# A trunk layer on one core: the output projection in seven products, its operand resident, the mix passed through DRAM, stages queued as one

## The chip, the core and the metric

The kernel runs on one core of one Trainium2 chip. It is written so that each instruction goes to one engine's queue: TensorE (PE, matmuls and transposes into PSUM banks), VectorE (DVE), ScalarE (ACT), GpSimd (POOL) and SyncE (SP), which issues most DMAs. A queue is served in order; engines meet through semaphores. The order in a queue is not simply that of the program: a scheduler lays the instructions out ahead of time by priority, and `tc.high_priority(offset=n)` moves what is written under it forward by n instructions' worth of priority. The metric is device time in microseconds of one execution, as the median of several runs. Before the change it is 1659.52 us (three runs, 1656.72 to 1660.0).

## The reference

One layer of a hybrid encoder trunk, 1024 tokens by 1024 features, all float32. The part around the change:

```python
mix = (jax.nn.sigmoid(gate_ret + merge_gate_b[l, 0]) * y_a
       + jax.nn.sigmoid(gate_lru + merge_gate_b[l, 1]) * y_b)
x = x + mix @ w_out[l]

h = rms_norm(x, norm2_w[l])
up = h @ ffn_w_up[l]
gate, val = jnp.split(up, [D_FF], axis=-1)
gate = causal_depthwise_conv(gate, ffn_conv_w[l], ffn_conv_b[l])
x = x + (jax.nn.gelu(gate) * val) @ ffn_w_down[l]
```

Ahead of it come an input projection with 28 column groups, a retention branch of four heads (y_a) and a recurrent branch with convolution and scan, the LRU (y_b). After it comes the last norm.

## The kernel before

**Precision.** [...] A product takes three passes, high by high, high by low and low by high (`PASSES`, line 129). A 128x128 block by a 128x512 row block is three matmuls.

**Units.** A projection is cut into jobs. A job has a left operand of four blocks A11, A12, A21, A22 (each 128 rows by four 128-wide pieces of k) and a right operand of sets B11 to B22 (each four tiles j of 128x512), which stays in SBUF for all jobs of the stage. A plain job (`mm_std`, line 346) makes the four quarters (m, h) of its output in 8 block products of 12 matmuls, 96 in all. A fast job (`mm_fast`, line 407) is Strassen's scheme in the form with seven products, 84 matmuls; it needs sums of A blocks (S1 to S4, made in `preps`, lines 265 to 291) and of B sets (T1 to T4, made once per stage). After a product that the scheme uses twice, ScalarE copies the bank out (L432, in `keep`), and VectorE adds what belongs together (L438, L443).

**Queues of work written out by hand.** `loads` (line 224) loads A blocks in the order of the list `queue`, and `preps` splits them; `pump` (line 296) drives both ahead of the products, up to seven blocks (`NBLK`). `builders` (line 307) is a list of generators that build right operands; `build` gives it a budget after each product, as long as 20 tiles of the pool U (81 tiles of 128x512) are free, and `need` forces it when a product lacks its set. `back` holds generators with background work of a stage (rotary, retention, LRU steps), driven by `advance`. `hp(SOON)` puts builders 400 ahead, `hp()` and `pump` 1500, the copies of `keep` and `total` 3000.

**Stages.** 28 jobs of the input projection; four plain jobs with w_ret_o (`emit_ret_o`); four with w_lru_o, the first plain, three fast (`emit_lru_o`, line 1068), whose output quarters are the rows of mix: channels 256n + 128m, tokens 512h. They stay in SBUF in `mixf`, 16 tiles. Then, lines 1194 to 1241, the output projection as plain loops: split the 16 tiles of mix; for each column half c load and split eight tiles of w_out, and for each of eight row tiles 24 matmuls (L1221), add x (L1223), store to `x1_d` (L1225). In the second column half each group of four row tiles goes through `norm_half` (line 533): the squares' sums, the scale per row (L537), 4 transposes per k tile (L543), and a split with the norm's weight (L547 to L553) into the operand `h2` of the next stage. Then 24 up jobs, the first plain (tokens in the free dimension, so `h2` sets B11 and B21 are tokens 0 to 511), with `post_ff` behind each, which stores gated channels into `ff_d` in blocks; the sums of h2 come from `tsets` (line 574). Then three groups of four down jobs: the A blocks are read from `ff_d`, the right operand w_dn is loaded by `operand` (line 1021), and its sums were made during the up stage by `down_sums` (line 1286), stored in `td_d` and read back by `down_op`. Each stage is appended to `queue` when its `run` is called (line 473).

`operand` holds a tile back until it has had time to land: `landed` (line 569) waits for two ticks (`LAG`), a tick being a call of `build`.

## Time and profile before

| what | value |
|---|---|
| runs | 1660.0, 1659.52, 1656.72 us; median 1659.52 |
| profiled execution | 1658.44 us; span from first to last instruction 1656.7 us |
| granted TensorE clock, mean | 0.997 |
| HBM | read 177.38 MB, written 67.11 MB |
| input projection, 0 to 653 us | TensorE busy 638.42 us, VectorE 531.38, ScalarE 393.02 |
| ret and LRU outputs, 653 to 844 | 186.51 of 191; 155.99; 110.32 |
| output projection, 844 to 938 | 92.75 of 94; 42.01; 22.46 |
| up, 938 to 1410 | 467.82 of 472; 372.45; 236.29 |
| down and end, 1410 to 1657 | 236.77 of 247; 185.22; 118.14 |

Times are microseconds from the first instruction. A row of a group reads: line, engine, operation, tiles written and read, shapes and count, then busy time and mean nanoseconds of one, then the idle time of the engine ahead of them with the instruction that ended most of it. A row of the timeline reads: start, length, engine, line, operation, count, and in brackets the idle time before it with its releaser. In the windows each engine has its busy time and its number of instructions; PEclk is the granted TensorE clock (1.00 is full), DMA the mean busy share of 16 DMA engines. Matmuls are pipelined, so a matmul's duration is longer than the distance between two of them.

### The profile page before, as it was taken

What the parts mean: (1) busy time and instruction counts of PE and PEld (TensorE: products, weight loads), DVE (VectorE), ACT (ScalarE), POOL (GpSimd) and SP (SyncE); (2) the same over time, 40 slices, a digit from 0 to 9 for tenths busy, and PEclk for the clock granted to TensorE, in tenths of its full rate; (3) what the DMA queues carried; (4) which work ended last, traced back from release to release, by engine and by line L of the source; (5) the groups of instructions that cost most, each with busy time, mean ns of one, the idle gap of its engine ahead of it and who ended that gap; (6) DMA issues with size and microseconds to landing.
All of it is one profiled execution on the core that took longest, in us unless ns stands there. A gap on an engine that the chain in (4) does not pass through costs nothing. (4 is left out here: it accounts for less than half of the span.)

```text
span 1656.7 us, 21338 instructions
## 1 busy us (share of the span) xinstructions
PE 1622.3 (98%) x7224; PEld 1329.8 (80%) x7224; DVE 1287.0 (78%) x2366; ACT 880.2 (53%) x1480; POOL 40.6 (2%) x60
## 2 busy tenths in 40 slices
PE   8999999999999998999999999999999999999997
PEld 6788888888888877888778778888888887888886
DVE  8998767676888888958871798777777767877786
ACT  7664444535677866853440464444444545453554
POOL 0001000000000000000000000000000000000000
PEclk9999999999999999999999999999999999999999
DMA  8243223131332337658462144444444456778761
GB/s 296 81 161 102 73 68 90 45 96 45 104 119 95 134 122 251 213 171 268 153 215 89 65 150 163 138 134 135 139 143 139 156 160 218 260 262 264 267 203 77
DMA packets 134350, 251.16 MB, mean 152 GB/s; under 512 B 15584, under 2 KB 15712, under 8 KB 134240
## 3 DMA queue, kind: packets, MB, share of 16 engines
q1 hardware_dynamic: 130016, 236.16, 43.9%
q0 software_dynamic: 4224, 13.64, 2.2%
q8 instruction: 56, 0.92, 0.2%
q14 instruction: 54, 0.44, 0.1%
HBM read 177.38 MB, written 67.11 MB: 148 GB/s over the span
## 5 line engine op out<-in xcount | busy, mean ns | idle before, releaser
L417 PE MATMUL g<-u,w 128*128 128x512 f32 x5124 | 1204.0, 393 | 14.9 <-ACT u L432 13.3
L417 PEld LDWEIGHTS g<-u,w 128*128 128x128 f32 x5124 | 958.2, 188 | 218.7 <-ACT u L432 18.6
L188 ACT CAST w<-w 128x512 fp32r<-128x512 f32 x471 | 291.3, 620 | 413.2 <-PE g L417 286.9
L189 DVE TENSOR_TENSOR w<-w,w 128x512 fp32r<-128x512 f32 x471 | 321.9, 684 | 83.4 <-ACT w L188 73.7
L360 PE MATMUL g<-u,w 128*128 128x512 f32 x960 | 223.5, 390 | 0.0
L360 PEld LDWEIGHTS g<-u,w 128*128 128x128 f32 x960 | 179.3, 188 | 38.0 <-ACT u L686 0.3
L443 DVE TENSOR_TENSOR u<-g,u 128x512 f32<-128x512 f32 x183 | 125.3, 685 | 50.5 <-PE g L417 40.4
L432 ACT COPY u<-g 128x512 f32<-128x512 f32 x183 | 106.1, 580 | 65.0 <-PE g L417 62.8
L122 DVE TENSOR_TENSOR u<-u,u 128x512 fp32r<-128x512 f32 (+1 forms) x192 | 122.0, 683 | 15.1 <-ACT u L122 10.4
L122 ACT CAST u<-u 128x512 fp32r<-128x512 f32 x160 | 90.4, 619 | 45.0 <-DVE u L122 15.3
L1221 PE MATMUL g<-u,u 128*128 128x512 f32 x384 | 90.0, 392 | 1.0 <-ACT u L188 0.9
L1221 PEld LDWEIGHTS g<-u,u 128*128 128x128 f32 x384 | 71.3, 188 | 16.6 <-ACT u L188 1.4
L1254 DVE SCALAR_TENSOR_TENSOR u<-u,par,u 128x511 f32<-128x511 f32 x96 | 71.6, 745 | 4.1 <-ACT u L1251 3.4
L1259 POOL DMA_DIRECT2D ff_d<-u x48 | 36.1, 752 | 1251.7 <-DVE u L1258 1251.7
L271 DVE TENSOR_TENSOR w<-w,w 128x512 f32<-128x512 f32 x61 | 42.0, 689 | 25.3 <-DMA w<-ff_d 9.6
L188 ACT CAST u<-u 128x512 fp32r<-128x512 f32 x72 | 43.3, 619 | 26.5 <-DMA u<-w_out 11.2
L1251 ACT ACTIVATE u<-u,par 128x512 f32<-128x512 f32 x48 | 39.2, 817 | 28.2 <-DVE u L443 27.5
L852 PE MATMUL a<-u,u 128*128 128x512 f32 x192 | 48.7, 393 | 2.5 <-ACT u L188 1.6
L189 DVE TENSOR_TENSOR u<-u,u 128x512 fp32r<-128x512 f32 x72 | 47.9, 683 | 4.0 <-ACT u L188 3.7
L1223 DVE TENSOR_TENSOR u<-g,u 128x512 f32<-128x512 f32 x16 | 10.9, 690 | 48.2 <-PE g L1221 48.2
L852 PEld LDWEIGHTS a<-u,u 128*128 128x128 f32 x192 | 35.5, 188 | 12.0 <-ACT u L188 3.1
L274 DVE TENSOR_TENSOR w<-w,w 128x512 f32<-128x512 f32 x61 | 41.9, 687 | 1.0
(175 smaller groups left out, 1211.7 us busy)
## 6 DMA issues: line engine op xcount, KB each, us to landing
w<-w_in SPq DMA_DIRECT2D x112, 256.0 KB, 2.7
w<-w_up SPq DMA_DIRECT2D x96, 256.0 KB, 2.7
u<-w_dn SPq DMA_DIRECT2D x96, 256.0 KB, 3.2
u<-x_d SPq DMA_DIRECT2D x56, 256.0 KB, 5.0
x_d<-u SPq DMA_DIRECT2D x48, 256.0 KB, 3.5
ff_d<-u POOLq DMA_DIRECT2D x48, 256.0 KB, 2.9
td_d<-u SPq DMA_DIRECT2D x48, 256.0 KB, 3.3
w<-ff_d SPq DMA_DIRECT2D x48, 256.0 KB, 4.3
```

The lines of the kernel that those rows point to most:

```text
L122: ins = fn(*args, **kw)
L188: S.copy(hi, src)
L189: V.tensor_sub(lo, src, hi.bitcast(F32))
L271: V.tensor_add(s1, a21, a22)
L274: V.tensor_sub(s1, s1, a11)
L360: PE.matmul(ps[h], w[a][:, c], o[b], start=n == 0, stop=n == 23)
L417: PE.matmul(bank, w[a][:, c], need(op, (bn, j))[b], start=first and n == 0, stop=n == 11, skip_group_check=True)
L432: BS.last = S.copy(u, bank).ins.name
L443: BV.last = V.tensor_add(u, bank, u).ins.name
L852: PE.matmul(ps, wg[g][a][:, cs], xs[k][b], start=q == 0, stop=q == 5)
L1221: PE.matmul(ps, o[a][:, 128 * t:128 * t + 128], wo[k][b], start=n == 0, stop=n == 23)
L1254: V.scalar_tensor_tensor(c[:, s:], src[:, :TH - s], w, c[:, s:], ALU.mult, ALU.add)
```

## The change

The output projection becomes a stage of jobs like the down stage. w_out is its right operand, resident in SBUF for all four jobs (tokens 256t + 128m are A's rows), with the sums T1 to T4 made during retention, stored to DRAM (`tw_d`) and read back. The quarters of mix are stored to DRAM in blocks (`mix_d`) and loaded as A blocks; a job's blocks are loaded only once the quarters are written out in the program (`ready`). The first job runs plain, in the new order `mm_by` "k" (all four quarters on k half 0, then all on half 1, in four banks); three are fast. The first up job runs `mm_by` "h" (token half 0 first). x1 goes to DRAM from each quarter, ScalarE squares it, and the norm becomes a generator, started after the third and the fourth output job, in the background. The up and down jobs are put into `queue` ahead of the output jobs' run.

```diff
+    def mm_by(jb, op):
+        r = range(2)
+        steps = ([(m, h, kh) for kh in r for m in r for h in r] if jb.by == "k" else
+                 [(m, h, kh) for h in r for kh in r for m in r])
...
+        for m, h, kh in steps:
+            an, bn = f"A{m + 1}{kh + 1}", f"B{kh + 1}{h + 1}"
...
+            pump((jb, an))
+            n = 0
+            for j in range(4):
+                c = slice(128 * j, 128 * j + 128)
+                o = need(op, (bn, j))
+                for a, b in PASSES:
+                    PE.matmul(banks[m, h], jb.blk[an][a][:, c], o[b], start=left[m, h] == 2 and n == 0,
+                              stop=left[m, h] == 1 and n == 11)
+                    n += 1
...
+            if not left[m, h]:
+                jb.emit(m, h, banks[m, h], None)
+                psg.put(banks[m, h])
+            build(BRATE)
+            advance(RATE)
...
     def loads():
...
             for nm in jb.order:
+                m, kh = int(nm[1]) - 1, int(nm[2]) - 1
+                while jb.ready is not None and not jb.ready(m, kh):
+                    yield None
                 t = W.get()
...
+    def out_w_sums(j):
+        def rd(kh, c):
+            t = get()
+            SY.dma_start(t, w_out[4 * kh + j, :, TH * c:TH * c + TH])
+            return t
+        b11, b12, b22 = rd(0, 0), rd(0, 1), rd(1, 1)
+        yield 1.0
+        V.tensor_sub(b11, b12, b11)
+        ST.dma_start(tw_d[0, j], b11)
+        V.tensor_sub(b12, b12, b22)
+        ST.dma_start(tw_d[2, j], b12)
+        put(b12)
+        b21 = rd(1, 0)
+        yield 1.0
+        V.tensor_sub(b22, b22, b11)
+        ST.dma_start(tw_d[1, j], b22)
+        put(b11)
+        yield 1.0
+        V.tensor_sub(b21, b21, b22)
+        ST.dma_start(tw_d[3, j], b21)
+        put(b21, b22)
...
+    def kept_sums(op, src):
+        def fetch(n, j):
+            t = get()
+            SY.dma_start(t, src[int(n[1]) - 1, j])
+            return t
+        keys = [(f"T{i}", j) for i in (1, 2, 3, 4) for j in range(4)]
+        for key, (tick, t) in zip(keys, reads(fetch, keys, AHEAD_B)):
+            yield from landed(tick)
+            op[key] = split(t, get, BS, BV)
+            put(t)
+            yield 0.6
...
             V.tensor_add(t, t, g)
             put(g)
-            mixf[ch, h] = t
+            ST.dma_start(mix_d[2 * h:2 * h + 2, :, ch // 4, :, ch % 4, :].rearrange("t m p c -> p (t m) c"),
+                         t.rearrange("p (q c) -> p q c", q=4))
+            put(t)
+            mixed.add((ch, h))
...
-            add(base + 2, emit_to(gg, AF.Silu, True), lambda hd=hd: ret_out(hd, dict(gg)))
+            add(base + 2, emit_to(gg, AF.Silu, True), lambda hd=hd: chain(ret_out(hd, dict(gg)), out_w_sums(hd)))
...
+    def emit_out(t, fast):
+        def emit(m, c, src, unit):
+            if fast and unit is not None:
+                acc = unit
+            else:
+                acc = wjobs[t].take(m, c)
+                V.tensor_add(acc, src, acc)
+                if unit is not None:
+                    put(unit)
+            i = 2 * t + m
+            ST.dma_start(x1_d[x_row(t, m, c)], acc)
+            j = psa.get()
+            S.activation(j, acc, AF.Square, accum_out=nst[:, c, i:i + 1])
+            psa.put(j)
+            if t == 3:
+                last4[m, c] = acc
+            else:
+                put(acc)
+        return emit
...
+            rstd_of(r, v, w)
+            if t >= 2:
+                return norm_half(t - 2)
...
+    def norm_half(half):
+        z = {}
+        for t in range(4):
+            i = 4 * half + t
+            for c in range(2):
+                z[t, c] = get()
+                if i < 6:
+                    SY.dma_start(z[t, c], x1_d[x_row(i // 2, i % 2, c)])
+        yield 1.0
...
+        for k in range(KT):
+            ps = psa.get()
+            for t in range(4):
+                c0 = 128 * (k % 4)
+                PE.transpose(ps[:, 128 * t:128 * t + 128], z[t, k // 4][:, c0:c0 + 128], ident)
+            w = pc("norm2_w", k)
+            hi, lo, f = get(F32R), get(F32R), get()
+            S.activation(hi, ps, AF.Copy, scale=w)
+            V.scalar_tensor_tensor(lo, ps, w, hi.bitcast(F32), ALU.mult, ALU.subtract)
+            S.activation(f, ps, AF.Copy, scale=w)
...
+            yield (0.5, 0.25)[half]
...
+        if half == 1:
+            builders.append(tsets(h2, lambda n, j: keep2[n, j], here=True))
...
+    def out_start():
+        builders.append(operand(wop, w_out_set, False, ("B11", "B12", "B21", "B22")))
+        builders.append(kept_sums(wop, tw_d))
+
+    wjobs = [Job(lambda m, kh, t=t: mix_d[t, m, kh].rearrange("p k c -> p (k c)"), wop,
+                 emit_out(t, t > 0), out_post(t), fast=t > 0, last=t == 3, drop12=t == 0,
+                 pre=((0, 0), (0, 1), (1, 1)), fetch=from_x(t), by=None if t else "k",
+                 order=None if t else ("A11", "A21", "A12", "A22"),
+                 ready=lambda m, kh, t=t: all((4 * kh + j, t // 2) in mixed for j in range(4)))
+             for t in range(4)]
+    ojobs[-2].post = out_start
+    queue.extend(wjobs)
...
+    ups = [Job(pair_src(w_up, i), h2, emit_to(gv), up_post(i), fast=i >= STD_U, last=i == NF - 1,
+               drop12=i == STD_U - 1, by="h" if i == 0 else None,
+               order=None if i else ("A11", "A21", "A12", "A22")) for i in range(NF)]
...
+                 ready=lambda m, kh, g=g: state["ff"] >= 8 * g + 4 * kh + 4)
              for g in range(3) for t in range(4)]
+    queue.extend(ups + djobs)
+    run(wjobs)
+    run(ups)
     run(djobs)
```

The old loops (lines 1194 to 1241) and the old `norm_half` are taken out; `down_op` calls `kept_sums` in place of its own copy of that loop.

173 lines of the change are left out of this document (73 added, 100 removed).

## The prediction

> **What bounds the kernel now.** I read the page first, then the windows, then TensorE's own timeline around the places where its work changes hands. The page gives the bound:
>
> ```profile
> span 1656.7 us, 21338 instructions
> PE 1622.3 (98%) x7224; PEld 1329.8 (80%) x7224; DVE 1287.0 (78%) x2366; ACT 880.2 (53%) x1480; POOL 40.6 (2%) x60
> L417 PE MATMUL g<-u,w 128*128 128x512 f32 x5124 | 1204.0, 393 | 14.9 <-ACT u L432 13.3
> L1221 PE MATMUL g<-u,u 128*128 128x512 f32 x384 | 90.0, 392 | 1.0 <-ACT u L188 0.9
> ```
>
> TensorE is idle for 1656.7 − 1622.3 = 34.4 us in all. So the change can act in two ways only: fewer matmuls, or more or less idle time at the hand-overs. The mean of 392 ns is a latency; the pitch has to be read where nothing stands in between. VectorE empties one bank per 24 matmuls in the old output stage, and waits for TensorE each time:
>
> ```profile
> 867.68 0.69 DVE L1223 TENSOR_TENSOR u<-g,u 128x512 f32<-128x512 f32 x1 [4.00 <-PE g L1221]
> 873.12 0.69 DVE L1223 TENSOR_TENSOR u<-g,u 128x512 f32<-128x512 f32 x1 [4.75 <-PE g L1221]
> 878.56 0.69 DVE L1223 TENSOR_TENSOR u<-g,u 128x512 f32<-128x512 f32 x1 [4.75 <-PE g L1221]
> ```
>
> The starts are 5.44 us apart, so one matmul costs 5.44 / 24 = 0.2267 us. The idle time that the change can touch is in these rows of TensorE (start, length, and in brackets the idle time before, with what ended it):
>
> ```profile
> 649.29 4.61 PE L417 MATMUL g<-u,w 128*128 128x512 f32 x12 [4.75 <-ACT u L432]
> 838.47 5.78 PE L417 MATMUL g<-u,w 128*128 128x512 f32 x24 [2.02 <-ACT u L432]
> 851.18 63.61 PE L1221 MATMUL g<-u,u 128*128 128x512 f32 x279 [0.95 <-ACT u L188]
> 941.60 0.74 PE L543 MATMUL a<-cst,u 128*128 128x128 f32 x4 [0.28 <-DVE u L537]
> 990.21 10.08 PE L417 MATMUL g<-u,w 128*128 128x512 f32 x43 [0.98 <-ACT u L432]
> 1396.48 3.06 PE L417 MATMUL g<-u,w 128*128 128x512 f32 x12 [1.11 <-ACT u L432]
> 1402.70 7.36 PE L417 MATMUL g<-u,w 128*128 128x512 f32 x24 [1.81 <-ACT u L432]
> ```
>
> The output stage starts at about 844 and ends near 937. It loses little itself; 2.02 us are lost in the last LRU unit just ahead of it, and 2.92 us where up hands over to down.
>
> **Part 1: fewer products.** The old loop issues 384 matmuls (2 column halves × 8 row tiles × 24). The new stage has four units: the first in eight products, 8 × 12 = 96, the other three in seven, 3 × 84 = 252, so 348. That removes 36 × 0.2267 = 8.16 us from an engine that has nothing to hide them behind. The first up unit keeps its 96 in another order, and the 64 transposes stay. This is the only large term. Whether the dense pitch survives in such a stage can be read from the down stage, which already has this very shape (one unit of 96, three of 84, operand and sums read back from DRAM), here with one hand-over between operands (1561 to 1584):
>
> ```profile
> core 0: us, PE busy (x) PEld busy (x) DVE busy (x) ACT busy (x) POOL busy (x), PEclk, DMA share, GB/s
> 819.00:844.00 25.00, 22.98 (x102) 18.67 (x101) 23.22 (x39) 16.32 (x30) 0.00 (x0) 1.00 0.72 228
> 938.00:960.00 22.00, 21.73 (x111) 17.46 (x110) 21.17 (x45) 13.05 (x23) 0.00 (x0) 1.00 0.22 72
> 960.00:990.00 30.00, 29.22 (x128) 23.18 (x126) 29.82 (x52) 17.84 (x30) 1.53 (x2) 1.00 0.40 129
> 1440.00:1482.00 42.00, 42.00 (x187) 34.79 (x186) 25.28 (x41) 15.83 (x29) 0.00 (x0) 1.00 0.78 256
> 1561.00:1584.00 23.00, 23.00 (x102) 18.77 (x101) 22.25 (x38) 17.54 (x33) 0.00 (x0) 1.00 0.92 306
> ```
>
> TensorE is busy for all 23.00 us while VectorE stands at 22.25 of 23 and the DMA engines at 0.92. So neither a full VectorE nor busy DMA engines cost time by themselves there.
>
> **Part 2: VectorE in the new stage.** One 128x512 operation costs 4.29 / 7 = 0.61 us back to back:
>
> ```profile
> 830.91 4.29 DVE L189 TENSOR_TENSOR u<-u,u 128x512 fp32r<-128x512 f32 x7
> ```
>
> From the start of the last LRU unit to the end of the first output unit TensorE has 84 + 96 = 180 matmuls, 40.8 us. VectorE has in it: that LRU unit's 3 totals and 8 merge operations, 32 splits of w_out and its sums, 4 splits of the first unit's blocks, 7 splits and 4 sums for the second, 4 additions: 62 × 0.61 = 38.0 us. It fits at 93%, and the last eight splits (T3, T4) are not needed for some 11 us more. From the third fast unit to the end of the first up unit there are 180 matmuls plus transposes, about 41 us plus 64 × 0.1 (an estimate from the 0.74 us for four in the row at 941.60, partly overlapped); VectorE has there seven bank operations, some 15 for blocks of up, the norm (16 scalings, 16 low parts) and 32 for the sums of h2: about 50 us, the last of it due only in the next up unit. The windows at 938 and 960 show the old kernel with VectorE equally full (21.17 of 22, 29.82 of 30), and TensorE losing 0.27 and 0.78 us. I take 0.5 us more than before for the norm's hand-over, from 0 to 5 (five being the excess of 50 us over the 46 or 47 that TensorE has, if all of it landed on it). Square moves from VectorE to ScalarE for half of the tiles, on an engine that is 53% busy: nothing.
>
> **Part 3: the mix through DRAM.** The mix splits go (16, hidden in the old stage too) and 16 stores plus 16 block loads come, all on SP. Blocks of k half 0 come from LRU units 0 to 1 and are early. The blocks A12 and A22 of output unit 0 need the (1,0) quarter of the very last LRU unit, which ends with its sixth product. Chain: product, add, store, load, split. Cover: the seventh product (12 matmuls) and the four first steps of unit 0 on k half 0 (48): 60 × 0.2267 = 13.6 us. The nearest rows:
>
> ```profile
> u<-x_d SPq DMA_DIRECT2D x56, 256.0 KB, 5.0
> x_d<-u SPq DMA_DIRECT2D x48, 256.0 KB, 3.5
> ff_d<-u POOLq DMA_DIRECT2D x48, 256.0 KB, 2.9
> w<-ff_d SPq DMA_DIRECT2D x48, 256.0 KB, 4.3
> DMA to landing us min/median/max: 2.5/3.4/6.9
> 843.15 0.68 DVE L1072 TENSOR_TENSOR u<-g,u 128x512 f32<-128x512 f32 x1
> 850.32 0.68 DVE L1073 TENSOR_TENSOR u<-u,u 128x512 f32<-128x512 f32 x1
> ```
>
> Best case 2 × 0.68 + 2.9 + 4.3 + two split halves (0.62 and 0.68) = 9.9 us: hidden by 3.7. But the old quarter's add ended at 851.0, though its product ended at 838.47 + 12 × 0.2267 = 841.2: 9.8 us, because VectorE was doing operand splits first. In the new kernel such splits stand at the same place, with a smaller head start (400 instead of 1500). With 9.8 for this part the chain is 9.8 + 7.2 + 1.3 = 18.3, a wait of 4.7 us. SP, whose queue stands still at that load until the store lands, then issues the reads of the sums late by as much; they have the rest of unit 0 as cover. I take 1.5 us of wait, nearer to the hidden end because the head start is smaller.
>
> [...] The mix is stored in runs of 128 floats, 512 bytes. If that doubled the store, the chain would grow by 2.9 us and the sum below by as much; the trace does not bear it out, as ff_d is stored in the same runs and lands in 2.9 us, against 3.5 for x_d in runs of 2 KB.
>
> **Part 4: loads of w_out.** The old kernel splits w_out as soon as a load is issued, and ScalarE stands in front of the transfer:
>
> ```profile
> ACT u L188 <- DMA u<-w_out: 7.6, 7, 1.8
> u<-w_out SPq DMA_DIRECT2D x16, 256.0 KB, 3.8
> ```
>
> That delays the copies (L432) for which TensorE waited 2.02 us at 838.47 and then 0.95 us at 851.18. The new loads go through the builder that holds each back two products (5.4 us, more than 3.8) before its split. I take the whole 2.97 us as gained; at worst none of it. In place of it, sums that come late for unit 1 (T1 at its second product): 0.5 us, between 0 and the 2.5 us or so that the lru hand-over lost in
>
> ```profile
> 786.71 0.96 PE L417 MATMUL g<-u,w 128*128 128x512 f32 x3 [0.95 <-ACT u L432]
> 788.27 2.60 PE L417 MATMUL g<-u,w 128*128 128x512 f32 x10 [0.59 <-ACT u L122]
> 791.78 44.67 PE L417 MATMUL g<-u,w 128*128 128x512 f32 x194 [0.92 <-DVE u L122]
> ```
>
> **Part 5: sums of w_out made during retention.** 16 loads, 16 subtractions, 16 stores, behind each head's ret_out. 16 × 0.61 = 9.8 us of VectorE, 32 issues of SP. Heads run from about 197 to 430:
>
> ```profile
> 180.00:330.00 150.00, 148.86 (x713) 122.93 (x712) 105.42 (x229) 68.26 (x124) 0.00 (x0) 1.00 0.24 71
> 330.00:460.00 130.00, 129.63 (x610) 106.84 (x609) 96.99 (x204) 66.70 (x113) 0.00 (x0) 1.00 0.27 84
> ```
>
> VectorE has 280 − 202 = 78 us free there and DMA share is a quarter: nothing, and up to 9.8 us if it were full. The background list becomes longer by 12 credits, so later LRU steps shift; that can move the 4.75 us wait at 649.29, which also slows the clock after it:
>
> ```profile
> 645.00:649.30 4.30, 0.01 (x1) 0.01 (x1) 0.53 (x2) 1.17 (x3) 0.00 (x0) 1.00 1.03 395
> 649.30:652.00 2.70, 2.70 (x7) 2.15 (x8) 2.70 (x6) 2.70 (x6) 0.00 (x0) 0.53 0.63 193
> 652.00:655.00 3.00, 3.00 (x13) 2.43 (x12) 1.73 (x4) 1.66 (x4) 0.00 (x0) 0.86 0.84 249
> ```
>
> The clock costs 2.70 × 0.47 + 3.00 × 0.14 = 1.7 us, so this place is worth 6.4 us either way. Nothing in the change aims at it: I take 0.
>
> **Part 6: stages queued together.** The down blocks may be loaded earlier. But they already are:
>
> ```profile
> L233 SPq DMA_DIRECT2D w<-ff_d x48: 319/323/689, 1373.2 to 1607.0; - x48
> ```
>
> The first goes out at 1373.2, 25 us before the waits at 1396 and 1402. Of their 2.92 us I take 0.5 as gained, from 0 to 2.92.
>
> **The sum**, against the profiled execution's own 1658.44 us: −8.16 −2.97 +1.5 +0.5 +0.5 −0.5 = −9.1, so 1649.3. The median of the three runs is 1659.52, 1.1 us above that execution; a median of the new kernel should be near 1650, which I give.
>
> **The rivals.** (a) The way through DRAM decides. If the add is late by 9.8 us and both transfers take the 6.9 us that the slowest ff_d landing took, the chain is 9.8 + 13.8 + 1.3 = 24.9 us, the wait 11.3, and with the slow clock after it (1.7) 13 us: 1658.4 − 8.2 + 13 = 1663. It turns slower once the chain passes 13.6 + 8.2 − 1.7, about 20 us. For it: SP is one queue in order, and the whole store, load and sums traffic falls together. Against it: the down hand-over at 0.92 DMA share with no idle.
> (b) VectorE falls behind at the norm and at T1: the upper ends 5 and 2.5 with no gain from w_out: 1658.4 − 8.2 + 7.5 − 0.5 = 1657.2, no change within what can be told. For it: 38.0 of 40.8 and 50 of 47. Against it: the windows at 938 to 990.
> (c) The hand-over at 649 falls into another order and its wait goes as well: 1649.3 − 6.4 = 1643.
> (d) Queuing together does nothing: 1649.8, which cannot be told from the forecast.
>
> **How the numbers follow.** This kernel's runs tell 0.2%, 3.3 us, from no change. Forecast with (d), 1645 to 1655: 0.56. (c): 0.08. (b) and milder cases of (a), 1655 to 1661: 0.16. (a) at its price, and the same place at 649 growing, 1662 to 1670: 0.20. Faster by over 0.2% is below 1656.2: 0.56 + 0.08 + 0.04 of the third = 0.68; the same 0.10; slower 0.22. The range for 8 in 10 runs from 1642 to 1664; the likeliest case's own is 1645 to 1655.
>
> **What would show it.** Right: 348 matmuls in the output units at 0.2267 us; no idle of TensorE beyond 2 us between 820 and 990; no ScalarE wait for w_out; in retention TensorE as busy as in the two windows above. Part 3 is wrong if the fifth step of the first output unit waits for a block's split whose load stood behind a mix store; Part 2 if the transposes of the second half wait for VectorE by more than 1 us. The forecast is wrong if a wait above 3 us, with a clock below 1, stands at either hand-over.

## The result and the profile after

The changed kernel takes 1662.78 us (median of 17 runs, 1659.48 to 1666.63) against 1660.0 us for the kernel before (17 runs, 1655.92 to 1663.68). The ratio is 1.0017, with a 95% interval from 1.0008 to 1.0026: it is slower, by 2.8 us or 0.17%, where 1650 was forecast and 0.2% was taken as the least that can be told from no change. The profiled execution took 1661.77 us, with a span of 1660.0.

From the page and the groups of TensorE of the changed kernel:

```profile
span 1660.0 us, 21593 instructions
PE 1616.7 (97%) x7188; PEld 1323.8 (80%) x7188; DVE 1317.6 (79%) x2418; ACT 913.9 (55%) x1543; POOL 40.7 (2%) x60
L407 PE MATMUL g<-u,w 128*128 128x512 f32 x192 | 49.7, 406 | 8.0 <-ACT w L191 7.7 <-DVE u L123 0.3
```

The 36 matmuls are gone (7224 to 7188), yet TensorE is busy only 5.6 us less, and it is idle for 1660.0 − 1616.7 = 43.3 us, where it was 34.4. L407 is the line of the plain products in the new order: one wait of 7.7 us ahead of a single matmul, for a split of a left block (L191). A split is two operations: ScalarE's cast to fp32r gives the high part (0.62 us at 835.12 below), VectorE's subtraction the low rest (0.69 us at 835.77). TensorE's timeline shows where the wait lies (start, length, count, and in brackets the idle time before):

```profile
650.83 5.73 PE L462 MATMUL g<-u,w 128*128 128x512 f32 x24 [3.65 <-ACT u L477]
...
840.43 7.21 PE L462 MATMUL g<-u,w 128*128 128x512 f32 x24 [2.33 <-ACT u L477]
847.48 10.14 PE L407 MATMUL g<-u,w 128*128 128x512 f32 x44
857.45 2.88 PE L462 MATMUL g<-u,w 128*128 128x512 f32 x12
868.04 12.48 PE L407 MATMUL g<-u,w 128*128 128x512 f32 x48 [7.71 <-ACT w L191]
...
1403.39 5.62 PE L462 MATMUL g<-u,w 128*128 128x512 f32 x24
...
1433.54 49.25 PE L462 MATMUL g<-u,w 128*128 128x512 f32 x216 [0.87 <-DVE u L1451]
1597.03 48.14 PE L462 MATMUL g<-u,w 128*128 128x512 f32 x204 [2.27 <-ACT u L477]
```

The 24 matmuls at 840.43 are the last two products of the last LRU unit, the 44 behind them (with four ahead) the four steps of output unit 0 on k half 0; the 12 at 857.45 are unit 1's first product, which TensorE had in its queue ahead of unit 0's fifth step, the first on k half 1. Then it stands until 868.04. Windows of the changed kernel at these places (stretch, then busy time of each engine, PEclk, DMA share, GB/s):

```profile
840.00:842.00 2.00, 1.57 (x4) 1.28 (x5) 2.00 (x5) 2.00 (x5) 0.00 (x0) 0.54 0.74 250
842.00:845.00 3.00, 3.00 (x12) 2.35 (x11) 3.00 (x6) 3.00 (x7) 0.00 (x0) 0.74 1.01 306
858.00:864.00 6.00, 2.33 (x11) 1.59 (x9) 4.34 (x7) 3.81 (x7) 0.00 (x0) 1.00 0.96 292
868.00:871.00 3.00, 2.96 (x7) 2.34 (x8) 2.58 (x5) 2.54 (x5) 0.00 (x0) 0.52 1.04 368
1390.00:1430.00 40.00, 40.00 (x176) 32.63 (x175) 37.56 (x65) 28.28 (x52) 3.02 (x4) 1.00 0.77 253
```

After both waits the granted clock is low, 0.54 and 0.74 from 840 to 845 and 0.52 from 868 to 871: the 24 matmuls take 7.21 us instead of 5.78 before, the 48 take 12.48, where 48 × 0.2267 and the same overhang of 0.34 make 11.22. The up to down hand-over, in the last row, has no wait left.

**The chain behind the 7.71 us** can be followed through three queues of the changed kernel, VectorE, ScalarE and SP:

```profile
835.77 0.69 DVE L192 TENSOR_TENSOR w<-w,w 128x512 fp32r<-128x512 f32 x1 [8.03 <-ACT w L191]
...
841.79 4.90 DVE L123 TENSOR_TENSOR u<-u,u 128x512 fp32r<-128x512 f32 x8
...
848.28 4.89 DVE L123 TENSOR_TENSOR u<-u,u 128x512 fp32r<-128x512 f32 x8
...
855.51 0.68 DVE L1129 TENSOR_TENSOR u<-g,u 128x512 f32<-128x512 f32 x1
...
856.71 0.68 DVE L1130 TENSOR_TENSOR u<-u,u 128x512 f32<-128x512 f32 x1
```

```profile
831.03 0.59 ACT L477 COPY u<-g 128x512 f32<-128x512 f32 x1 [7.76 <-PE g L462]
835.12 0.62 ACT L191 CAST w<-w 128x512 fp32r<-128x512 f32 x1 [3.49 <-DMA w<-mix_d]
835.64 4.26 ACT L123 CAST u<-u 128x512 fp32r<-128x512 f32 x8
839.80 0.57 ACT L477 COPY u<-g 128x512 f32<-128x512 f32 x1
...
867.37 1.24 ACT L191 CAST w<-w 128x512 fp32r<-128x512 f32 x2 [1.87 <-DMA w<-mix_d]
```

```profile
857.79 1.03 SPq L1132 DMA_DIRECT2D mix_d<-u  x2
862.02 0.33 SPq L1079 DMA_DIRECT2D u<-tw_d  x1
862.45 0.38 SPq L1263 DMA_DIRECT2D u<-x  x1
863.57 0.37 SPq L1132 DMA_DIRECT2D mix_d<-u  x1
864.22 1.81 SPq L238 DMA_DIRECT2D w<-mix_d  x4
```

Read from the top. ScalarE has its copy done at 831.62 and then stands until 835.12 at the split of a block, by its place in the queue one of output unit 1, whose load from mix_d has not landed; it was issued at 828.43 and takes 6.6 us. VectorE stands behind it for 8.03 us. The eight splits of w_out that come next on ScalarE start at 835.64 without a wait of their own. When the block has come, the splits of w_out and of its sums (L123) run in a burst, ahead of the merges (L1129, L1130) that the (1,0) quarter of mix needs. Its product, the twelfth of the 24 matmuls at 840.43, ends at about 844 (the clock is 0.54 and 0.74 there); its add ends at 857.39, 13.4 us later. The store of that quarter is the second of the two in SP's row at 857.79. It is issued at 858.4 and lands 5.8 us later, at 864.16, and its landing lets the load of the block go at 864.22 (the store's time to landing, then SP's wait ahead of the load):

```profile
DMA to landing us min/median/max: 5.8/5.8/5.8
SPq L238 <- DMA mix_d<-u: 0.2, 1, 0.2
```

In between SP stands at a read of the sums of w_out, because the slot that it fills is still being read by an earlier store of mix (3.1 us in SP's waits). But SP is through with that read and what follows it by 863.94, so the order of its queue adds next to nothing to this chain. What is long is the store: in the window from 858 to 864 above the DMA engines are at 0.96, and reads of the sums and of x were issued just ahead of it. The load lands 3.1 us after its issue, and the split lets TensorE go 0.7 us after the split's start. From the end of the product: 13.4 to the end of the add, 1.0 to the store's issue, 5.8, 3.1 and 0.7 make 24.0 us. TensorE's cover is the 13.6 us of the prediction and 2.7 for the 12 matmuls of unit 1, which leaves the 7.7 us.

**Where the time went, up to the first down product** (at 1399.37 in the timeline of before and at 1402.25 after, 1.14 us ahead of the row at 1403.39: 2.9 us later). Gone: 8.16 of products, the waits of 2.02, 0.95 and 1.11. New: 2.33 and 0.32 in the LRU unit with 1.4 of slow clock, 7.71 with 1.3 of slow clock, and 2.17 instead of 0.98 in the norm's hand-over (four waits from 970 to 985, of 0.22, 0.85, 0.39 and 0.71). Sum: −12.2 + 13.1 + 1.2 = +2.1. The other 0.8 us is what is left of gains and losses ahead: TensorE comes to the hand-over near 649 2.6 us later than before, with waits of 1.41 and 1.33 in retention where there were 0.90 and none, and gets most of it back there, with 1.1 us less of wait and no slow clock. From there to the end both take the same, 257.3 and 257.8 us: the wait of 1.81 and its slow clock (7.36 us for 24 matmuls before, 5.62 now) are gone in this profile, and a new wait of 0.87 at 1433.54 and one of 2.27 at 1597.03, where it was 0.97, with a slow clock after it (204 matmuls in 48.14 us, before 46.53), give it back.

### The profile page after: what moved, and what is told of

It reads as the page before. It is cut to its first block, busy times and chain, and to the rows that moved or that the text cites. A ratio compares the mean times of both kernels' runs of the same rounds, so it can differ in the third digit from the quotient of the medians.

```text
span 1660.0 us, 21593 instructions
## 1 busy us (share of the span) xinstructions
PE 1616.7 (97%) x7188; PEld 1323.8 (80%) x7188; DVE 1317.6 (79%) x2418; ACT 913.9 (55%) x1543; POOL 40.7 (2%) x60
## 4 chain that ended last, share of the span: by engine, by line
PE 53%; DVE 5%; DMA 4%; ACT 2%; issue 1%; SPq 0%; DVEq 0%; ACTq 0%
PE g L462 42%; PE g L367 7%; PE g L407 2%; PE a L871 2%; DVE u L123 1%; DMA y_d<-u 1%; DVE w L192 1%; DMA u<-og_d 1%; DMA w<-ff_d 1%; ACT u L123 1%; DMA mix_d<-u 0%; DMA u<-t_d 0%; DMA u<-sg_d 0%; DVE u L904 0%; PE a L1320 0%
## 5 line engine op out<-in xcount | busy, mean ns | idle before, releaser
L462 PE MATMUL g<-u,w 128*128 128x512 f32 x5376 | 1262.4, 393 | 14.1 <-ACT u L477 9.9
L462 PEld LDWEIGHTS g<-u,w 128*128 128x128 f32 x5376 | 1005.2, 188 | 227.4 <-ACT u L477 14.0
L191 ACT CAST w<-w 128x512 fp32r<-128x512 f32 x496 | 307.0, 621 | 437.5 <-PE g L462 337.2
L192 DVE TENSOR_TENSOR w<-w,w 128x512 fp32r<-128x512 f32 x496 | 339.5, 686 | 94.8 <-ACT w L191 89.4
L367 PE MATMUL g<-u,w 128*128 128x512 f32 x864 | 199.5, 389 | 0.0
L367 PEld LDWEIGHTS g<-u,w 128*128 128x128 f32 x864 | 161.9, 188 | 34.4 <-DVE u L123 0.3
L488 DVE TENSOR_TENSOR u<-g,u 128x512 f32<-128x512 f32 x192 | 131.8, 686 | 57.9 <-PE g L462 47.6
L123 DVE TENSOR_TENSOR u<-u,u 128x512 fp32r<-128x512 f32 (+1 forms) x224 | 142.4, 686 | 14.9 <-ACT u L123 11.6
L477 ACT COPY u<-g 128x512 f32<-128x512 f32 x192 | 111.6, 581 | 68.7 <-PE g L462 63.1
L123 ACT CAST u<-u 128x512 fp32r<-128x512 f32 x192 | 108.0, 618 | 53.7 <-DMA u<-tw_d 11.8
L278 DVE TENSOR_TENSOR w<-w,w 128x512 f32<-128x512 f32 x64 | 44.1, 689 | 22.3 <-DMA w<-w_up 9.2
L407 PE MATMUL g<-u,w 128*128 128x512 f32 x192 | 49.7, 406 | 8.0 <-ACT w L191 7.7
L407 PEld LDWEIGHTS g<-u,w 128*128 128x128 f32 x192 | 36.0, 193 | 16.4 <-ACT w L191 8.1
L281 DVE TENSOR_TENSOR w<-w,w 128x512 f32<-128x512 f32 x64 | 44.1, 688 | 1.0
L287 DVE TENSOR_TENSOR w<-w,w 128x512 f32<-128x512 f32 x64 | 43.9, 686 | 0.4
L294 DVE TENSOR_TENSOR w<-w,w 128x512 f32<-128x512 f32 x64 | 43.9, 686 | 0.4
L1370 DVE TENSOR_TENSOR u<-u,u 128x512 f32<-128x512 f32 x48 | 33.1, 689 | 6.7 <-ACT u L1369 6.7
```

Source lines behind the costliest of these rows:

```text
L123: ins = fn(*args, **kw)
L191: S.copy(hi, src)
L192: V.tensor_sub(lo, src, hi.bitcast(F32))
L278: V.tensor_add(s1, a21, a22)
L281: V.tensor_sub(s1, s1, a11)
L367: PE.matmul(ps[h], w[a][:, c], o[b], start=n == 0, stop=n == 23)
```

## The experiments

The theory after this reading: the mix comes late from DRAM because VectorE reaches the merges late; the seven products themselves are worth their 8 us. Its rivals were that the cost is in the way through DRAM whatever VectorE does, that the sums of w_out, which seven products need, cost what the products save, and that the stages queued together or the sums made in retention cost time elsewhere. Ratios are to the kernel before, run on the same chip as the experiment; they come from all runs and can differ a little from the ratio of the medians. 0.001 is 1.66 us. "Plain" below means that all four output units run in eight products and the sums of w_out, still made in retention, are not read back.

| run | output units | median us (runs) | ratio [95%] |
|---|---|---|---|
| the changed kernel | 1 plain, 3 in seven | 1662.78 (17) | 1.0017 [1.0008, 1.0026] |
| e1, merges first | same | 1656.81 (9) | 0.9966 [0.9955, 0.9978] |
| e10, e1 plain | plain | 1657.31 (12) | 0.9982 [0.9967, 0.9996] |
| e14, e1 without sums | 1 plain, 3 in seven | 1648.95 (6) | 0.9938 [0.9922, 0.9955] |
| e2, no late quarter | same | 1651.83 (5) | 0.9946 [0.9934, 0.9958] |
| e11, e2 plain | plain | 1653.04 (6) | 0.9941 [0.9924, 0.9958] |
| e13, e2 without sums | 1 plain, 3 in seven | 1645.56 (6) | 0.9916 [0.9897, 0.9936] |
| e6, e1 with unit 1's splits behind | same | 1658.2 (12) | 0.9987 [0.9978, 0.9997] |
| e8, e6 plain | plain | 1656.08 (11) | 0.9975 [0.9965, 0.9985] |

### e1: the merges of the last LRU unit first

```diff
-            V.tensor_mul(g, ps, g)
+            with (hp(NOW) if n == 3 else nullcontext()):
+                V.tensor_mul(g, ps, g)
...
```

(the add and the store with it)

> The changed kernel with the merges of the last LRU unit (mul, add, store of mix) put 3000 ahead in priority, so VectorE does them before the splits of w_out; the loads, blocks and data are the same. Theory A (the 7.7 us wait of the first output unit comes from the order in VectorE's queue: the merges of a product that ended at 843 are done at 853 to 857 behind some 24 operand splits): the wait at the start of its k half 1 falls below 1.5 us, the clock after it stays at 1.00, and the time falls by 7 to 10 us against the changed kernel, to 1650 to 1655. Theory B (the transfers decide: store, SP's queue and load alone take over 10 us): at least 4 us of the wait stay and the time falls by less than 4 us.

Measured: 1656.81 us, 6 us below the changed kernel (8.5 by the ratios). The 7.71 us wait is gone, and nothing stands at the fifth step. But the waits ahead of it have grown. ScalarE and TensorE of this run:

```profile
840.28 0.62 ACT L191 CAST w<-w 128x512 fp32r<-128x512 f32 x1 [5.02 <-DMA w<-mix_d]
840.80 4.26 ACT L123 CAST u<-u 128x512 fp32r<-128x512 f32 x8
```

```profile
841.47 0.49 PE L407 MATMUL g<-u,w 128*128 128x512 f32 x1 [1.39 <-ACT u L123]
842.28 0.96 PE L407 MATMUL g<-u,w 128*128 128x512 f32 x3 [0.31 <-DVE u L123]
845.60 8.20 PE L462 MATMUL g<-u,w 128*128 128x512 f32 x24 [2.36 <-ACT u L477]
853.64 21.02 PE L407 MATMUL g<-u,w 128*128 128x512 f32 x92
```

VectorE's order was a cause, as the theory had it. The second cause is seen in the first fence: ScalarE's queue is headed by a split of a block that lands just before 840.28, with eight splits of w_out that TensorE needs behind it; that costs 1.39 + 0.31 + 2.36 us of waits and 8.20 − 5.6 = 2.6 us of slow clock.

### e2: output unit 0 does not wait for the last quarter

```diff
-    wjobs = [Job(lambda m, kh, t=t: mix_d[t, m, kh].rearrange(...), wop,
+    wjobs = [Job(lambda m, kh, t=t: mix_d[t, m, kh if t else 0].rearrange(...), wop,
...
-                 ready=lambda m, kh, t=t: all((4 * kh + j, t // 2) in mixed for j in range(4)))
+                 ready=lambda m, kh, t=t: all((4 * (kh if t else 0) + j, t // 2) in mixed for j in range(4)))
```

> The changed kernel in which the first output unit reads its blocks of k half 1 from the places of k half 0, which were written long before; that leaves the second half of the sum out for its tokens. Nothing in it waits for the last LRU unit's merges. It bounds what the way through DRAM costs. If that wait and the slow clock after it are the whole loss: 9 us less than the changed kernel, near 1653, and TensorE idle below 1.5 us at that place. If the loss lies elsewhere (VectorE too full, sums late, the norm), the idle time moves to the next unit and less than 4 us are gained.

Measured: 1651.83 us, 11 us below the changed kernel. All transfers are still there; only the lateness is gone. (The edit leaves half of the sum out for unit 0's tokens.) TensorE of this run goes from the LRU unit into the output stage without a stop:

```profile
844.68 21.02 PE L407 MATMUL g<-u,w 128*128 128x512 f32 x92
865.54 5.60 PE L462 MATMUL g<-u,w 128*128 128x512 f32 x24
872.91 27.41 PE L462 MATMUL g<-u,w 128*128 128x512 f32 x118 [1.77 <-ACT u L477]
```

ScalarE does not stand at a block there either: unit 0's loads are not held back, and those behind them go out earlier too, six blocks by 825.11 where the changed kernel has four by 831.42. The late quarter and ScalarE's stand are thus taken away together, and together they are worth about 11 us of the miss of 13. The rest of the sum might now be thought right, as 1651.8 is within the likeliest case's own range; the pairs further down show that it is not.

### e4: the down jobs queued late again

```diff
-    queue.extend(ups + djobs)
+    queue.extend(ups)
```

> The changed kernel with the down jobs put into the queue only when their own run starts, as before the change. My forecast's reading (their loads were early anyway): within 2 us of the changed kernel. The rival (queuing together removed the 1.1 and 1.8 us waits at the hand-over from up to down): those waits come back and the time rises by 2 to 4 us.

Measured: 1666.26 us (10 runs), 1.0038 [1.0026, 1.005], 3.5 us above the changed kernel. Its profile has small waits in the down stage instead of the ones before the change (0.33 at 1418.74, 0.24 at 1421.75), and 3.40 instead of 2.27 at 1602.49; from the first down product on, this accounts for some 1.2 us; the rest lies ahead of it. Queuing together does not cost time; how much it gains is taken up in e15.

### e5: the sums of w_out made in retention, in the kernel before

```diff
-            add(base + 2, ..., lambda hd=hd: ret_out(hd, dict(gg)))
+            add(base + 2, ..., lambda hd=hd: chain(ret_out(hd, dict(gg)), out_w_sums(hd)))
```

> The kernel of before with only the sums of w_out added behind each head (16 loads, 16 subtractions, 16 stores; nobody reads them). My forecast's reading (hidden in retention): within 1 us of before. The rival (they displace background work, and the new waits of 1.4 and 1.3 us at 205 and 418 us in the changed kernel come from them): 2 to 4 us more than before, with waits of TensorE between 180 and 440 us above 2.5 us in all, against 1.4 before.

Measured: 1659.31 us (11 runs), 0.9999 [0.999, 1.0008]. Making the sums costs no time that these runs can tell (±1.5 us). The waits that the rival named are in its profile, 2.7 us between 180 and 440 (1.26 at 205.02 and 1.07 at 417.60 the largest), but TensorE then waits 3.08 us at the hand-over near 649 instead of 4.75.

### e6, e7: the splits of output unit 1's blocks put behind

```diff
-                jb.blk[nm] = split(src, W.get)
+                jb.blk[nm] = split(src, W.get, BS, BV) if jb.behind else split(src, W.get)
```

(`behind` is set for unit 1 alone: its splits then go behind ScalarE's last copy out of a bank; e6 on top of e1, e7 on the changed kernel alone)

> The run with the merges first, and besides the splits of the second output unit's blocks put behind ScalarE's last copy of a bank (an order in the queue, no wait). In the run with the merges first ScalarE stood 5.0 us at 835 to 840 in front of such a split whose block had not landed, though the second unit starts 40 us later, with eight operand splits behind it whose data were there; TensorE lost 1.39, 0.31 and 2.36 us at 841 to 846. If that split is the cause: these 4 us fall below 1.5 and the time is 3 to 4 us below the run with the merges first, 1652 to 1654, within 2 us of the run without the way through DRAM. If the operand splits are simply too many for ScalarE and VectorE there: the waits stay above 3 us and the time within 1.5 us of the run with the merges first.

> The changed kernel with only the second edit: the splits of the second output unit's blocks behind ScalarE's last copy, the merges where they were. If the split that stood in front of ScalarE's queue is the root (it made the operand splits late, and these the merges): the wait of 7.7 us falls below 1.5 us and the time to 1652 to 1655 without any priority for the merges. If the merges' place in VectorE's queue is a cause of its own: they come 4 us earlier at most, at least 3 us of the wait stay, and the time is 1656 to 1660.

Measured: e6 1658.2 us; e7 1659.36 us (12 runs), 0.9998 [0.9988, 1.0008]. In e6 the waits from 841 to 846 are gone, and two others stand in their place; in e7 the waits ahead of it are gone too, and the wait for the fifth step is longer than in the changed kernel (first row e7, the others e6, TensorE):

```profile
866.25 12.93 PE L407 MATMUL g<-u,w 128*128 128x512 f32 x48 [10.29 <-ACT w L191]
```

```profile
858.11 11.49 PE L407 MATMUL g<-u,w 128*128 128x512 f32 x48 [2.07 <-ACT w L191]
877.35 47.01 PE L462 MATMUL g<-u,w 128*128 128x512 f32 x199 [3.90 <-ACT u L477]
```

What is late now is the store. In e6 SP's queue reads:

```profile
842.21 0.42 SPq L1133 DMA_DIRECT2D mix_d<-u  x1
842.68 5.65 SPq L1079 DMA_DIRECT2D u<-tw_d  x4
848.42 0.39 SPq L1133 DMA_DIRECT2D mix_d<-u  x1
...
849.45 0.46 SPq L1133 DMA_DIRECT2D mix_d<-u  x1
...
854.31 2.22 SPq L238 DMA_DIRECT2D w<-mix_d  x5
```

The adds that the fifth step needs are done before 846 in this run, but four reads of the sums stand ahead of the next store for 5.7 us, so that the store of the (1,0) quarter goes out at 849.45, 3.75 us after its add. It then takes 4.8 us to land, and the loads go at 854.31, when it has. e7 is 3.2 ± 2.2 us below the changed kernel by the ratios: ScalarE's order alone takes the wait of 2.33 us and its slow clock away (24 matmuls in 5.67 us at 837.60), but not the one at the fifth step, as long as the merges are late. The two are separate causes. The reads of the sums, in SP's queue and on the DMA engines, are a third suspect.

### e8, e10, e11: four plain output units

```diff
-        builders.append(kept_sums(wop, tw_d))
...
-                 emit_out(t, t > 0), out_post(t), fast=t > 0, last=t == 3, drop12=t == 0,
-                 pre=((0, 0), (0, 1), (1, 1)), fetch=from_x(t), by=None if t else "k",
+                 emit_out(t, False), out_post(t), last=t == 3, fetch=from_x(t), by=None if t else "k",
```

> The run with both edits, but all four output units in eight products (96 matmuls each, 384 as before the change) and the sums T of w_out not read back. It prices the seven products by themselves. If the 36 matmuls are worth their pitch (36 x 0.2267): 8.2 us more than the run with both edits, near 1661. If the sums, the blocks' sums and the extra bank operations eat part of it: 3 to 6 us more. If more than 10, the plain units wait somewhere.

> The run with the merges first, with all four output units in eight products and no sums read back. With both edits the plain form was 2 us faster than the seven products, though it has 36 matmuls (8.2 us) more. If that holds for the form as such (the sums' splits and bank copies cost TensorE as much in waits as the products save): 1654 to 1658 here, within 2 us of the run with the merges first. If it came from the second edit, which made the fast units wait: 1662 to 1665.

> The run without the way through DRAM (first unit reads k half 0 twice, second half of the sum left out for its tokens), with all four units in eight products. It prices the seven products where nothing else waits. If the seven products keep their worth there: 8 us more than 1651.8, near 1660. If they are given back in waits: 1652 to 1656.

Measured: 1656.08, 1657.31 and 1653.04 us; none is 8 us above its partner in seven products. Three pairs now differ in eight against seven products, 36 matmuls or 8.16 us of TensorE, and in what seven need: the sums of w_out read back and split, sums of the blocks, copies of banks. e6 and e8 ran side by side on one chip; the other two pairs are compared across chips, through the ratios. By the ratios seven products change e8 to e6 by +2.0 us, e10 to e1 by −2.7, e11 to e2 by +0.8; with the half widths of both intervals combined as the root of their squares, the uncertainties are 2.3, 3.1 and 3.5 us. The mean is nothing, within 1.7. The saving that the forecast rests on is there in the count of matmuls and not in the time.

### e13, e14: seven products without the sums

```diff
-        builders.append(kept_sums(wop, tw_d))
+        def no_sums():
+            for i in (1, 2, 3, 4):
+                for j in range(4):
+                    wop[f"T{i}", j] = wop["B22", j]
+            yield 0.1
+        builders.append(no_sums())
...
```

(every sum is the set B22, so the output stage's values are left out; the part not shown keeps that set from being given back more than once)

> The run without the way through DRAM, in which the fast output units use the set B22 in place of every sum T: the 16 reads and 32 split operations of the sums are left out, and the output stage's values with them; the 348 matmuls and the bank copies stay. Without the way through DRAM the seven products were worth 1.2 us by medians and 3.5 by the profiles, not 8.2. If the sums' reads and splits crowd VectorE, ScalarE and SP there: TensorE's waits between 860 and 925 (1.77 and 0.57) vanish and the time falls by 2 to 5 us, to 1647 to 1650. If the fast form itself (bank copies and additions between products) is what waits: the 1.77 stays and the time is within 1 us of 1651.8.

> The run with the merges first, with the sums T left out in the same way (all four T sets are the set B22, so the output stage's values are left out). The way through DRAM is whole. If the sums' reads and splits are what the way through DRAM and ScalarE's queue run into: the waits between 835 and 900 (1.39, 0.31, 2.36, 1.05) fall below 2 us in all and the time to 1650 to 1653. If not, only 1 us or less is gained, and the waits are ScalarE's in front of the early block, which stays.

Measured: 1645.56 and 1648.95 us. Against the same kernels with the sums (e2, e1) that is 5.0 ± 3.8 and 4.6 ± 3.3 us less by the ratios (6.3 and 7.9 by the medians). Against the same kernels in plain products (e11, e10) it is 4.1 ± 4.3 and 7.3 ± 3.7 us less, so both agree with 8.16, and the second does not agree with nothing. TensorE in e14 shows one wait in the LRU unit, which is more than the 2 us that its expectation allowed, without a slow clock, and none in the output units:

```profile
841.90 5.74 PE L462 MATMUL g<-u,w 128*128 128x512 f32 x24 [2.36 <-ACT u L479]
...
868.33 31.89 PE L462 MATMUL g<-u,w 128*128 128x512 f32 x140
```

e13 came out below its forecast time, but not by the mark that was named: its wait in the output units grew, to 3.37 us at 875.20 where e2 has 1.77, and its profiled execution, the second slowest of its six runs, is only 0.7 us below that of e2. So its gain stands in the times alone.

Taken together, the 16 reads and the 32 operations that split the sums, all at the start of the output stage, cost about 5 us of the 8.16 that the seven products save. In that price is also the room that the sums take in the pool of tiles, which e13 and e14 leave free. What costs the rest, the sums of blocks and the copies of banks, was not tried by itself.

### e9, e12: the reads of the sums from another queue

```diff
-            SY.dma_start(t, src[int(n[1]) - 1, j])
+            Q.dma_start(t, src[int(n[1]) - 1, j])
```

(Q is GpSimd's queue for w_out's sums; e9 on top of e1, e12 with `behind` for units 1 to 3 besides)

> The run with the merges first, and the reads of the sums T issued from GpSimd's queue in place of SP's; the queue of SP then holds nothing that waits for a free tile between the mix stores and the block loads. In the earlier runs SP stood 2.3 to 5.7 us at such reads, with a mix store or a block load next in line. If SP's order is what keeps the way through DRAM long: the first unit's block loads go out 3 us earlier or more, TensorE has no wait above 1 us at that unit's k half 1, and the time is at or below the run with the merges first (1653 to 1657). If not: the waits stay as they are and the time within 1 us of 1656.8; if GpSimd's reads are slower, the sums come late and the second unit waits more than 2 us.

> The reads of the sums from GpSimd's queue, merges first, and the block splits of the second to fourth output unit behind ScalarE's last bank copy. It removes the three places seen so far: the merges behind splits, SP in front of a read, ScalarE in front of a block that has not landed. If these three are all of the loss at the start of the output stage: TensorE's waits between 835 and 900 below 2 us in all, and 1650 to 1654. If each cure only moves the wait: above 3 us there and 1655 to 1659.

Measured: e9 1662.62 us (12 runs), 1.0004 [0.9989, 1.0018]; e12 1659.54 us (12 runs), 0.9985 [0.9974, 0.9997]. Neither beats e1. SP no longer stands at these reads, and the waits move on (TensorE in e9):

```profile
842.17 7.35 PE L462 MATMUL g<-u,w 128*128 128x512 f32 x24 [2.35 <-ACT u L477]
...
883.37 46.36 PE L462 MATMUL g<-u,w 128*128 128x512 f32 x194 [5.82 <-DVE u L1274]
```

In e12 the first of these is gone, and 7.11 us stand at 860.76. SP's order is out of the way, but the transfers are longer: the mix store that the load of the block waits for is issued at 848.50 in e9 and lands 9.1 us later, where in e1 it takes 2.3. From 835 to 845 the DMA engines are at 1.02 in e9 and at 0.82 in e1. So the queue that issues the reads is not what makes the sums dear; that it is the transfers, all at once on the same DMA engines, fits these rows but was not tried alone.

### e3: the sums' start tied to the last load of unit 0

```diff
-        builders.append(kept_sums(wop, tw_d))
+        def sums():
+            while "A22" not in wjobs[0].raw:
+                yield 0
+            yield from kept_sums(wop, tw_d)
+        builders.append(sums())
```

> The changed kernel in which the reads and splits of the sums T of w_out start only once the first output unit's blocks of k half 1 have been asked for; merges and priorities as in the changed kernel. If VectorE's order is the cause: 14 of the 24 splits no longer stand ahead of the merges, the merges end some 8 us earlier, the wait of 7.7 us falls below 2 us, the time by 5 to 8 us against the changed kernel, unless the sums then come late for the second unit (a new wait there of up to 4 us, and the gain 2 to 5). If transfers decide: the wait stays above 4 us.

Measured: 1663.18 us (10 runs), 1.0025 [1.0013, 1.0037], with 8.77 us at 868.72. The condition holds in the order in which the program is written, and the load is written early; the scheduler's order on the queues came out as in the changed kernel. It is a repeat of that kernel and says nothing about later sums.

### e15: the stages queued together, in the kernel before

```diff
+    queue.extend(ups + djobs)
+    run(ups)
     run(djobs)
```

(with `ready` for the down jobs, as in the change)

> The kernel of before with only the down jobs put into the queue together with the up jobs, with the same readiness rule; nothing else. It prices part 6 by itself. My forecast's 0.5 us: no change that can be told from before. The reading of the late-queue run, where undoing it cost 3.5 us: the waits of 1.11 and 1.81 us at the hand-over from up to down go, and 3 to 4 us are gained, 1656 to 1657.

Measured: 1658.9 us (11 runs), 0.9992 [0.9979, 1.0006]: by the time, no change that can be told. TensorE of this run at the hand-over from up to down:

```profile
1400.32 1.30 PE L364 MATMUL g<-u,w 128*128 128x512 f32 x5
1401.46 5.63 PE L421 MATMUL g<-u,w 128*128 128x512 f32 x24
```

The waits of 1.11 and 1.81 us are gone here too, and the 24 matmuls take 5.63 us, not 7.36. In this profile the stretch from the first down product to the end is 254.3 us, against 257.3. The one profile shows 3 us, the eleven runs 1.3 (−3.5 to +1.0 by the interval), e4 3.5 in the changed kernel, 1.2 of it in that stretch: a gain of 0 to 3 us.

### A better version

e1 and e8 compute the whole layer and stand below both kernels: 1656.81 and 1656.08 us. What e8 keeps of the change is the resident w_out, the mix through DRAM and the stages queued together, with the merges first and unit 1's splits behind; it keeps none of the seven products.

## Why the prediction was wrong

**The step that failed is Part 3**, "I take 1.5 us of wait, nearer to the hidden end because the head start is smaller". The mechanism was named and its mark came true word for word: the fifth step waited for a split whose load stood behind a mix store, and at that place rival (a) had the kernel at 1662 to 1670, with a chance of 0.20. But its size was 7.71 us and 1.3 of slow clock; with ScalarE's stand it is 11 us (e2). The chain that Part 3 added up for late merges, 18.3 us with a wait of 4.7, had 9.8 us to the add, 2.9 for the store and 4.3 for the load; measured were 13.4, 1.0 until the store was issued, 5.8 and 3.1. Taking 1.5 in place of the 4.7 rested on the head start alone. Rival (a)'s sum of 24.9 us came near the measured 24.0 partly by luck: it had the add at 9.8 and both transfers at 6.9, so one term was too short and another too long. That smaller head start did not keep the splits behind the merges; e1, which turns that order by a priority, gains 6 us. The stores of mix_d, in runs of 512 bytes, land in 4.4 us at the median in the changed kernel, those of x_d, in runs of 2 KB, in 3.8: these medians show no doubling. The one store on the chain did take twice the 2.9 us (5.8), but with the DMA engines at 0.96, and no run here tells short runs and busy engines apart.

**Part 1 failed too, behind other errors**: "an engine that has nothing to hide them behind … the only large term". The matmuls went, but what seven products need was priced in other parts as small change: the reads with "the rest of unit 0 as cover", the splits in a budget, the lateness as 0.5. The pairs with eight and seven products put the worth of the whole at 0, each within 2 to 3.5 us; without the sums it is 4 to 7, each within about 4. The window taken as evidence, the down hand-over with VectorE at 22.25 of 23, reads sums as well, but the blocks of its first unit do not come from a product just finished. That e2 still came near the forecast is owed to gains that were put too low: e11 saves no product, and is 7.6 us below the kernel before (9.8 by the ratio), and its profile has no wait of TensorE from 800 to 970 and none between up and down.

**Part 2's budget was right and its use wrong.** 38.0 of 40.8 us says that VectorE can do the work, not that it does it in an order that fits: it stood for 8.03 us behind one block and was late by 13.4 with one add. Part 2's own mark, transposes that wait for VectorE by more than 1 us, did not come true (0.42, for ScalarE); the norm's hand-over cost 1.2 us more than before, where 0.5 was forecast, within the 0 to 5 given.

**Part 4 was right for its cause and wrong for its gain.** ScalarE waits for no load of w_out any more (VectorE does, 4.9 us in all, in retention). But the copies that TensorE waited for are still late, 2.33 and 0.32 us where it was 2.02 and 0.95, because ScalarE now stands at a block of mix (3.49 us ahead of 835.12). The gain of 2.97 did not arrive; in e2, where no block is late, TensorE has no wait there.

**Part 5 was right in time**: 0.9999, though new waits in retention show in the profiles. The hand-over at 649 stayed, with 3.65 instead of 4.75, so rival (c) is out.

**Part 6** took 0.5 of 2.92 because the first load was early. Both waits went, with the slow clock, but the gain in time is 0 to 3 us: what the changed kernel gained by it in the down stage was lost again, in its profile, at 1433 and 1597.

What stays open: why the runs of e15 show less than its profile, and whether the sums could be read late enough to cost nothing. e3 was meant for that and did not try it. Open too is how much of the length of the mix store is the traffic of the sums' reads on the DMA engines, and what in the seven products, besides those sums, costs the rest of the 8.16 us.

## What to carry to other kernels

A scheme that saves matmuls is priced together with the operands that it needs, at the place where they are made: here, at a hand-over, all that seven products needed cost as much as the 36 matmuls that they saved (8.16 us, within 1.7), about 5 us of it the reads and splits of the sums. A budget that fits tells that an engine is fast enough, not that its queue is in the right order; look for the first instruction in it that waits for a transfer, and count what stands behind it. What the next stage's first load depends on belongs ahead of any prefetch, in each queue that it passes, and curing one queue shows the next. Before a queue's stand is called the cause, look at what released the instruction behind it: here it was the landing of a store, not the end of SP's stand.

## What the hardware showed

The same length of wait slowed the clock in one run and not in another. The clock at the hand-over near 650, in the changed kernel and in e2 (TensorE's timeline, then the window):

```profile
651.00:654.00 3.00, 3.00 (x14) 2.47 (x15) 3.00 (x7) 3.00 (x7) 0.00 (x0) 1.00 0.71 216
```

```profile
650.24 8.63 PE L462 MATMUL g<-u,w 128*128 128x512 f32 x24 [2.78 <-ACT u L477]
651.00:654.00 3.00, 3.00 (x9) 2.33 (x8) 3.00 (x6) 2.30 (x5) 0.00 (x0) 0.50 0.58 175
```

The changed kernel waited 3.65 us there and went on at full clock (24 matmuls in 5.73 us); e2 waited 2.78 us and had half the clock (8.63). In e14 a wait of 2.36 us at 841.90 left the clock alone (1.00 from 842 to 848, 24 matmuls in 5.74 us), and in e1 the same wait behind two shorter ones did not (0.50 from 845 to 848, 24 matmuls in 8.20 us). So in these runs the length of a wait alone does not tell whether a slow clock follows. Where it came it cost 1.3 us (868.04) to 2.9 us (8.63 in e2 against 5.73 in the changed kernel), the latter as much as the wait itself. What else decides it was not shown.
